# Value products of a hybrid trunk: two 144-column products joined into one of 288, the low part copied and added behind

## The chip, the cores and the metric

The kernel runs on one core of a Trainium2 chip. The metric is the device time of one execution in microseconds (us); lower is better. TensorE (PE) multiplies, VectorE (DVE), ScalarE (ACT) and GpSimd (POOL) do the elementwise work, SyncE (SP) starts the DMA transfers.

## The reference

A trunk of two layers with 2048 channels over 256 frames, with 16 learned tokens put ahead of them: T = 272 tokens. Layer 0 runs gated linear attention (GLA: 4 heads, key width 256, value width 512) and stick-breaking attention (8 heads of width 128) side by side; layer 1 is a Mamba-2 mixer. Each layer ends in a residual sum and a layer norm. What matters here is the last product of every head of layer 0, scores times values:

```python
# GLA, in chunks of 64 tokens
scores = jnp.where(causal, einsum('bcthk,bcshk->bchts', q_dec, k_inv), 0.0)
o_intra = einsum('bchts,bcshv->bcthv', scores, v)
...                                  # state of earlier chunks: o_inter
o_gla = _rms_norm_groups(o_intra + o_inter, norm_w, GLA_HEADS) * silu(gr)
# stick-breaking, in query blocks of 128
w = jnp.where(mask, exp(log_sigmoid(z) + log_between), 0.0)
outs.append(einsum('bhqk,bhkd->bhqd', w, v))
...
o_sb = outs * silu(sr)
mix = concatenate([o_gla, o_sb]);  f = mix @ w_out
```

All of it is in float32.

## The kernel before

Every large float32 product is made of three products of rounded parts: a value is split into a high part (rounded to the type fp32r by a copy on ACT) and a low part (the rest, by a subtraction, mostly on DVE). `three` (L178 to L180) then runs high times high, weights high times activations low, and weights low times activations high, each with 128 x 128 weights and 272 columns. PSUM, in which the products accumulate, holds four buffers "pj" for projections, two buffers "po" and two banks "z" for scores.

The weights of both layers come from HBM in units of 1 MB ("raw", three buffers, started by SP). ACT makes "whi" of each half (L159), DVE or POOL "wlo" (L160), five buffers each. PE runs through these units in a fixed plan: layer 0's projections, then its output product (activations "mixh", "mixl"), then layer 1. "dtgvh" and "dtgvl" are such parts of a small weight of layer 1's step sizes, split ahead of time; `hacc` (L449) is the running sum of layer 0's output.

The attention of layer 0 is side work: generators, one a head, of which a step is put between the projections' products. A scheduler then sets the final order of the instructions on each engine from its own estimate of times and from which buffers are free, so a change in one function moves instructions elsewhere too.

A head's side work, as far as it is touched here:

- its values are turned into rows of tokens through a DMA to DRAM and back ("vt"), and split into "gvh" and "gvl", two tiles of 128 tokens each (`to_tokens`, L617 to L622); tokens that don't fit, 16 at a chunk's edge, go to a small tile "v" together with their score parts "s".
- scores are made in a bank z, copied to "spad" on ACT (GLA: a plain copy; stick-breaking: an exponential, L821) and masked on POOL (L249, three selections).
- `parts_of` (L567 to L578) splits spad into "s0h" (ACT, L572) and "s0l" (DVE, L573), 432 columns: 16 for the small tile, 272 for key tile 0 and 144 for key tile 1. Key tile 1 bears only on the last 144 tokens.
- `values` (L629 to L638) adds up one block of 128 value channels in a po buffer: for key tile 0 three products of 272 columns (gvh by s0h, gvh by s0l, gvl by s0h), for key tile 1 the same three with 144 columns into columns 128 to 272 of po, and one product of 16 columns. It is called four times in each GLA head (`mix_gla`) and once in each stick-breaking head: 24 times.
- behind it, in a GLA head, DVE multiplies po by the gate ("gu", L733) and ACT squares it for the norm ("gsq", "gs", L735 and L738); POOL adds the squares (L739). In a stick-breaking head DVE multiplies po by the gate ("sby", L838), ACT makes mixh (L839) and DVE mixl (L840). The last of these heads, number 7, ends the inputs of layer 0's output product.

Of the kernel before, what the change touches and what calls it, by code (L numbers as in the profile page):

```python
# [6 lines left out]
F32 = mybir.dt.float32  # L7
F32R = mybir.dt.float32r
AF = mybir.ActivationFunctionType
ALU = mybir.AluOpType  # L10
PSUM = bass.MemoryType.PSUM

P = 128
# [6 lines left out]
T = NM + S  # L20
# [62 lines left out]
def _wait(*tasks):  # L83
    for t in tasks:
        while not t.done:
            yield


class _Body:
# [477 lines left out]
    def parts_of(self, src, stack=None, rows=()):  # L567


        n = src.shape[-1]  # L570
        p = [self.lp.tile([P, 432], F32R, tag=t, name=self.nm(t), bufs=2)[:, :n] for t in ("s0h", "s0l")]
        self.nc.scalar.activation(p[0], src, AF.Copy)  # L572
        self.nc.vector.tensor_tensor(p[1], src, p[0].bitcast(F32), op=ALU.subtract)  # L573
        for i, r in enumerate(rows):
            a = stack[32 * i : 32 * i + 16]
            b = p[r][:16, 0:16].rearrange("p (a b) -> p a b", a=1).broadcast_to([16, a.shape[1], 16])
            self.nc.vector.tensor_copy(a, b)
        return p  # L578
# [47 lines left out]
        lp = self.lp  # L626
        return [lp.tile([P, 2, 512], F32R, tag=n, name=self.nm(n), bufs=2) for n in ("gvh", "gvl")] + [self.v2[h % 2]]

    def values(self, o, vh, vl, v2, c, sh, sl, s2):  # L629

        mm = lambda r, a, b, start=False, stop=False: self.nc.tensor.matmul(  # L631
            o[:, r], a, b, start=start, stop=stop, skip_group_check=True
        )
        for t, r, w in ((0, slice(0, T), slice(16, 288)), (1, slice(128, T), slice(288, 432))):
            mm(r, vh[:, t, c], sh[:, w], start=t == 0)
            mm(r, vh[:, t, c], sl[:, w])
            mm(r, vl[:, t, c], sh[:, w])
        mm(slice(256, T), v2[:, c], s2[:, 0, :], stop=True)  # L638

    def post_gv(self, ps, h, j):  # L640
        lp = self.lp
# [61 lines left out]
    def mix_gla(self, h):  # L703
        nc, lp = self.nc, self.lp
        act, vec, mm = nc.scalar.activation, nc.vector, nc.tensor.matmul
        q, k = self.cur["q", h], self.cur["k", h]
        v = self.cur["v", h]
        g = self.cur["r", h]
        yield from _wait(self.tasks["r", h], *[self.tasks["v", h, j] for j in (1, 3)])

        zb = self.zbank()
        for j in range(2):
            mm(zb[:, 16:288], k[:, j, 0:128], q[:, j, 0:272], start=j == 0, stop=j == 1)
        for j in range(2):
            mm(zb[:, 288:432], k[:, j, 128:256], q[:, j, 272:416], start=j == 0, stop=j == 1)
        for j in range(2):
            mm(zb[:16, 0:16], k[:, j, 256:272], q[:, j, 416:432], start=j == 0, stop=j == 1)
        yield
        s = self.spad
        act(s, zb[:, :432], AF.Copy)  # L720
        self.causal(s[:, 16:144], 128, False)
        self.causal(s[:, 288:416], 128, False)
        self.causal(s[:16, 0:16], 16, False)
        yield
        st = self.s2[h % 2]
        sh, sl = self.parts_of(s, st, (0, 0, 1))
        yield
        u = lp.tile([P, 4, T], F32, tag="gu", name=self.nm("gu"))
        sq = lp.tile([P, T], F32, tag="gsq", name=self.nm("gsq"))
        for j in range(4):  # L730
            o = self.po()
            self.values(o, *v, slice(j * P, (j + 1) * P), sh, sl, st)
            vec.tensor_tensor(u[:, j, :], o[:, :T], g[:, j, :], op=ALU.mult)  # L733
            if j == 0:
                act(sq, o[:, :T], AF.Square)  # L735
            else:
                s2 = lp.tile([P, T], F32, tag="gs2", name=self.nm("gs2"), bufs=2)
                act(s2, o[:, :T], AF.Square)  # L738
                nc.gpsimd.tensor_tensor(sq, sq, s2, op=ALU.add)  # L739
            yield  # L740
        yield
        qh, ql = self.parts_of(sq)
        yield
        ms = self.po()
        mm(ms[:, :T], self.ones_r, qh, start=True, stop=False)
        mm(ms[:, :T], self.ones_r, ql, start=False, stop=True)
        yield
        m = lp.tile([P, T], F32, tag="gs2", name=self.nm("gms"), bufs=2)
        r = lp.tile([P, T], F32, tag="grs", name=self.nm("grs"))
        vec.tensor_scalar(m, ms[:, :T], 1.0 / GDV, RMS_EPS, op0=ALU.mult, op1=ALU.add)  # L750
        act(r, m, AF.Ln)
        act(r, r, AF.Exp, scale=-0.5)
        self.newton(r, m, sq)
        yield
        mh, ml = self.mix_tile(h)
        for j in range(4):
            vec.scalar_tensor_tensor(u[:, j, :], u[:, j, :], self.col(C_GN, 4 * h + j), r, op0=ALU.mult, op1=ALU.mult)
            act(mh[:, j, :], u[:, j, :], AF.Copy)
            vec.tensor_tensor(ml[:, j, :], u[:, j, :], mh[:, j, :].bitcast(F32), op=ALU.subtract)
            yield  # L760
# [23 lines left out]
    def mix_sb(self, h, q, k, v):  # L784
        nc, lp = self.nc, self.lp
        act, vec, mm = nc.scalar.activation, nc.vector, nc.tensor.matmul
        zb = self.zbank()
        gk = dict(skip_group_check=True)

        for a, b in ((0, 0), (0, 1), (1, 0)):  # L790
            mm(zb[:, 16:288], k[:, a, 0:128], q[:, b, :], start=a == b, stop=False, **gk)
        for a, b in ((0, 0), (0, 1), (1, 0)):
            mm(zb[:, 288:432], k[:, a, 128:256], q[:, b, 128:T], start=False, stop=False, **gk)
        for a, b in ((0, 0), (0, 1), (1, 0)):
            mm(zb[:16, 0:16], k[:, a, 256:T], q[:, b, 256:T], start=False, stop=False, **gk)
        yield

        sp = e = lp.tile([P, 432], F32, tag="ge", name=self.nm("sbe"))
        act(e, zb[:, :432], AF.Abs)
        act(e, e, AF.Exp, scale=-1.0)  # L800
        act(e, e, AF.Ln, bias=self.b_one)
        vec.scalar_tensor_tensor(sp[:, :432], zb[:, :432], 0.0, e, op0=ALU.max, op1=ALU.add)
        yield
        self.causal(sp[:16, 0:16], 16, True)
        self.causal(sp[:, 16:144], 128, True)
        self.causal(sp[:, 288:416], 128, True)
        yield
        sph, spl = self.parts_of(sp, self.sp2, (0, 1))
        yield

        for s in (sph, spl):
            mm(zb[:, 16:432], self.nL_r, s[:, 16:432], start=False, stop=False, **gk)
        for s in (sph, spl):
            mm(zb[:, 144:288], self.nones_r, s[:, 288:432], start=False, stop=False, **gk)

        last = zb[:, 144:432].rearrange("p (a c) -> p a c", a=2)[:, :, 128:144]
        mm(last, self.nones_r, self.sp2, start=False, stop=False, **gk)
        mm(zb[:16, 0:16], self.nL2[:, 0, :], self.sp2[:, 0, :], start=False, stop=True, **gk)
        yield
        w = self.spad  # L820
        act(w, zb[:, :432], AF.Exp)  # L821
        self.causal(w[:, 16:144], 128, True)
        self.causal(w[:, 288:416], 128, True)
        self.causal(w[:16, 0:16], 16, True)
        yield
        s2 = self.s2[h % 2]
        wh, wl = self.parts_of(w, s2, (0, 0, 1))
        yield
        while ("sv", h) not in self.tasks:
            yield  # L830
        yield from _wait(self.tasks["sv", h], self.tasks["sr", h // 4])
        o = self.po()
        self.values(o, *v, slice(0, P), wh, wl, s2)
        yield
        j, g = h % 4, 4 + h // 4
        mh, ml = self.mix_tile(g) if j == 0 else self.mix[g]
        y = lp.tile([P, T], F32, tag="gs2", name=self.nm("sby"), bufs=2)
        vec.tensor_tensor(y, o[:, :T], self.cur["sr", h // 4][:, j, :], op=ALU.mult)  # L838
        act(mh[:, j, :], y, AF.Copy)  # L839
        vec.tensor_tensor(ml[:, j, :], y, mh[:, j, :].bitcast(F32), op=ALU.subtract)  # L840
        yield
# [637 lines left out]
```

## Time and profile before

| | |
|---|---|
| median of 3 runs | 1376.98 us (1376.84, 1376.98, 1377.29) |
| the profiled execution | 1376.89 us, span 1375.2 us |
| mean granted clock of PE in it | 0.999 |
| PE busy | 1366.5 us, 99%, 10603 products |
| weight loads of PE (PEld) | 1318.6 us, 96% |
| DVE busy | 1033.6 us, 75%, 1763 instructions |
| ACT busy | 769.9 us, 56%, 1149 instructions |
| POOL busy | 263.5 us, 19%, 253 instructions |
| DMA | 256.73 MB, mean 187 GB/s |

The span runs from the first to the last event of the profiled execution; the execution's own time is 1.7 us longer. Products are pipelined in PE, so their records overlap: what one costs is the step from the end of the product ahead to its own end. A row of the timeline gives start and duration in us, engine, line, operation, output <- inputs, shape, and in brackets an idle time ahead of it with what ended it. L12 is line 12 of the kernel.

### The profile page before, as it was taken

To read this page: it belongs to the slowest core of one execution; us is meant where nothing else is said; L and a number is where in the kernel's file an instruction comes from. 1 tells how busy PE (TensorE), PEld (TensorE's weight loads), DVE (VectorE), ACT (ScalarE), POOL (GpSimd) and SP (SyncE) were. 2 spreads that over 40 slices of the span, in tenths; PEclk is the share of its full clock that TensorE was granted. 3 is DMA by queue.
4 is the path that set the end of the run, shared out by engine and by line. 5 is a ranking of instruction groups with operands and counts; after the bars stand their busy time and mean duration, and the time that the engine had idled before them with its cause. 6 is when DMAs were issued, how large, how long until landed. Compare 5 with 4: busy or idle time off the path is not lost.

```text
span 1375.2 us, 26163 instructions
## 1 busy us (share of the span) xinstructions
PE 1366.5 (99%) x10603; PEld 1318.6 (96%) x10603; DVE 1033.6 (75%) x1763; ACT 769.9 (56%) x1149; POOL 263.5 (19%) x253
## 2 busy tenths in 40 slices
PE   9999999999999999999999999999999999999998
PEld 8999999999999999999999999899898999989986
DVE  7858576576565574568899999887877879877687
ACT  6646455355345544556587676656565655656551
POOL 0000010100001100004400143331422323133221
PEclk9999999999999999999999999999999999999999
DMA  9656446446545454554355655565645565555561
GB/s 333 198 184 196 171 162 209 157 166 208 178 155 188 149 189 166 198 168 142 137 190 172 239 203 204 180 238 184 214 173 202 185 200 218 172 196 185 184 214 62
DMA packets 61945, 256.73 MB, mean 187 GB/s; under 512 B 26176, under 2 KB 29056, under 8 KB 33408
## 3 DMA queue, kind: packets, MB, share of 16 engines
q1 hardware_dynamic: 61104, 254.27, 53.7%
q8 instruction: 83, 1.36, 0.4%
q10 hardware_dynamic: 720, 0.79, 0.2%
q14 instruction: 38, 0.31, 0.1%
HBM read 249.29 MB, written 5.74 MB: 185 GB/s over the span
## 4 chain that ended last, share of the span: by engine, by line
PE 91%; DVE 6%; issue 1%; DMA 1%; ACT 0%; POOL 0%; SPq 0%; ACTq 0%; DVEq 0%; POOLq 0%
PE pj L178 25%; PE pj L179 25%; PE pj L180 24%; PE pj L494 4%; PE pj L496 4%; PE pj L495 4%; DVE wlo L160 1%; PE po L631 1%; PE po L1255 1%; DVE M L1125 1%; DMA raw<-in_wts 0%; DVE M L1126 0%; PE po L1194 0%; DVE M L1153 0%; DVE xt L1070 0%
## 5 line engine op out<-in xcount | busy, mean ns | idle before, releaser
L178 PE MATMUL pj<-xhi,whi 128*128 128x272 f32 (+4 forms) x2560 | 732.1, 286 | 1.2 <-DVE fix L956 0.5
L179 PE MATMUL pj<-xlo,whi 128*128 128x272 f32 (+4 forms) x2560 | 730.5, 286 | 0.0
L180 PE MATMUL pj<-xhi,wlo 128*128 128x272 f32 (+4 forms) x2560 | 729.8, 285 | 0.0
L159 ACT ACTIVATE whi<-raw 128x1024 fp32r<-128x1024 f32 (+2 forms) x434 | 449.2, 1038 | 379.9 <-PE pj L179 315.2
L160 DVE TENSOR_TENSOR wlo<-raw,whi 128x1024 fp32r<-128x1024 f32 (+2 forms) x405 | 503.7, 1248 | 197.5 <-ACT whi L159 192.0
L178 PEld LDWEIGHTS pj<-xhi,whi 128*128 128x128 f32 x2560 | 481.9, 188 | 3.7 <-ACT whi L159 1.5
L179 PEld LDWEIGHTS pj<-xlo,whi 128*128 128x128 f32 x2560 | 482.0, 188 | 1.7 <-issue 0.6
L180 PEld LDWEIGHTS pj<-xhi,wlo 128*128 128x128 f32 x2560 | 482.2, 188 | 0.4 <-issue 0.4
L178 PE MATMUL pj<-mixh,whi 128*128 128x272 f32 x384 | 110.9, 290 | 0.0
L180 PE MATMUL pj<-mixh,wlo 128*128 128x272 f32 x384 | 110.5, 288 | 0.0
L179 PE MATMUL pj<-mixl,whi 128*128 128x272 f32 x384 | 110.4, 288 | 0.0
L160 POOL TENSOR_TENSOR wlo<-raw,whi 128x1024 fp32r<-128x1024 f32 x29 | 73.7, 2541 | 190.5 <-ACT whi L159 175.7
L494 PE MATMUL pj<-whi,yh 128*128 128x512 f32 (+1 forms) x240 | 93.2, 388 | 0.0
L495 PE MATMUL pj<-wlo,yh 128*128 128x512 f32 (+1 forms) x240 | 92.6, 386 | 0.0
L496 PE MATMUL pj<-whi,yl 128*128 128x512 f32 (+1 forms) x240 | 92.2, 386 | 0.0
L261 POOL TENSOR_TENSOR gr<-gr,gsc 128x1088 f32<-128x1088 f32 x6 | 15.4, 2572 | 302.7 <-ACT gsc L260 302.7
L179 PEld LDWEIGHTS pj<-mixl,whi 128*128 128x128 f32 x384 | 72.4, 188 | 0.2
L178 PEld LDWEIGHTS pj<-mixh,whi 128*128 128x128 f32 x384 | 72.1, 188 | 0.4 <-ACT mixh L839 0.2
L180 PEld LDWEIGHTS pj<-mixh,wlo 128*128 128x128 f32 x384 | 72.3, 188 | 0.0
L503 DVE SCALAR_TENSOR_TENSOR acc<-pj,rr,acc 128x512 f32<-128x512 f32 (+1 forms) x65 | 46.5, 734 | 13.7 <-PE pj L496 13.5
L496 PEld LDWEIGHTS pj<-whi,yl 128*128 128x128 f32 x240 | 45.1, 188 | 9.1
L494 PEld LDWEIGHTS pj<-whi,yh 128*128 128x128 f32 x240 | 45.1, 188 | 8.9
(345 smaller groups left out, 1454.3 us busy)
## 6 DMA issues: line engine op xcount, KB each, us to landing
raw<-in_wts SPq DMA_DIRECT2D x212, 1024.0 KB, 4.9
ebc<-edr SPq DMA_DIRECT2D x8, 1664.0 KB, 6.6
raw<-in_wts SPq DMA_DIRECT2D x9, 256.0 KB, 5.9
vdr<-vt SPq DMA_DIRECT2D x8, 256.0 KB, 4.7
vt<-vdr SPq DMA_DIRECT2D x32, 64.0 KB, 2.4
hacc<-in_xT SPq DMA_DIRECT2D x7, 272.0 KB, 5.3
early<-in_wts SPq DMA_DIRECT2D x2, 512.0 KB, 6.4
vdr<-vt SPq DMA_DIRECT2D x8, 128.0 KB, 3.5
```

The lines of the kernel that those rows point to most:

```text
L159: self.nc.scalar.activation(hi, src, AF.Copy)
L160: eng.tensor_tensor(lo, src, hi.bitcast(F32), op=ALU.subtract)
L178: mm(ps, whi, xhi, start=first, stop=False)
L179: mm(ps, whi, xlo, start=False, stop=False)
L180: mm(ps, wlo, xhi, start=False, stop=last)
L261: mul(c, c, e, op=ALU.mult)
L494: mm(ps, yh[:, kk, tt], hi[:, k, :], start=kk == 0, stop=False)
L495: mm(ps, yh[:, kk, tt], lo[:, k, :], start=False, stop=False)
L496: mm(ps, yl[:, kk, tt], hi[:, k, :], start=False, stop=kk == 3)
L503: self.nc.vector.scalar_tensor_tensor(a, ps, r[:, t : t + 1], a, op0=ALU.mult, op1=ALU.add)
L631: mm = lambda r, a, b, start=False, stop=False: self.nc.tensor.matmul(o[:, r], a, b, start=start, stop=stop, skip_group_check=True)
L1125: vec.tensor_scalar(M[:, h, 0:256], eb[:, h, 0:256], self.est[:, 0, 0, gh : gh + 1], 0.0, op0=ALU.subtract, op1=ALU.min)
```

## The change

In `values`, key tile 1's two products with gvh as weights, one by the high and one by the low scores, become one product of 2 x 144 = 288 columns. Its output goes to two pieces of the po buffer: the high scores' part to columns 128 to 272 as before, the low scores' part to columns 368 to 512. Then ACT copies the low part to a tile "vlo" (one buffer), and DVE adds it to columns 128 to 272 of po. So that one operand holds both score parts, `parts_of` puts them in the two halves of one tile "s0" in place of two tiles. The area that is kept for dynamic DMA descriptors is set to 128.

```diff
     def parts_of(self, src, stack=None, rows=()):
-        p = [self.lp.tile([P, 432], F32R, tag=t, name=self.nm(t), bufs=2)[:, :n] for t in ("s0h", "s0l")]
+        p = self.lp.tile([P, 2, 432], F32R, tag="s0", name=self.nm("s0"), bufs=2)[:, :, :n]
+        p = [p[:, 0, :], p[:, 1, :], p]
...
-    def values(self, o, vh, vl, v2, c, sh, sl, s2):
+    def values(self, o, vh, vl, v2, c, s, s2):
         mm = lambda r, a, b, start=False, stop=False: self.nc.tensor.matmul(
-            o[:, r], a, b, start=start, stop=stop, skip_group_check=True
+            r, a, b, start=start, stop=stop, skip_group_check=True
         )
-        for t, r, w in ((0, slice(0, T), slice(16, 288)), (1, slice(128, T), slice(288, 432))):
-            mm(r, vh[:, t, c], sh[:, w], start=t == 0)
-            mm(r, vh[:, t, c], sl[:, w])
-            mm(r, vl[:, t, c], sh[:, w])
-        mm(slice(256, T), v2[:, c], s2[:, 0, :], stop=True)
+        w = slice(16, 288)
+        mm(o[:, :T], vh[:, 0, c], s[:, 0, w], start=True)
+        mm(o[:, :T], vh[:, 0, c], s[:, 1, w])
+        mm(o[:, :T], vl[:, 0, c], s[:, 0, w])
+        two = o[:, 32:512].rearrange("p (a x) -> p a x", a=2)[:, :, 96:240]
+        mm(two, vh[:, 1, c], s[:, :, 288:432])
+        mm(o[:, 128:T], vl[:, 1, c], s[:, 0, 288:432])
+        mm(o[:, 256:T], v2[:, c], s2[:, 0, :], stop=True)
+        e = self.lp.tile([P, 144], F32, tag="vlo", name=self.nm("vlo"))
+        self.nc.scalar.activation(e, two[:, 1], AF.Copy)
+        self.nc.vector.tensor_tensor(two[:, 0], two[:, 0], e, op=ALU.add)
...
-    nc = bacc.Bacc("TRN2", target_bir_lowering=False, num_devices=1)
+    nc = bacc.Bacc("TRN2", target_bir_lowering=False, num_devices=1, dynamic_dma_scratch_size=128)
```

The three callers of `parts_of` and the two of `values` take the new forms, and lines behind `parts_of` move down by 1, those behind `values` by 6 to 7: the products are L632 now, the copy is L644, the add L645, sby L845 and mixh L846.

Over the whole program PE has 24 products fewer, ACT 24 copies and DVE 24 adds more; the orders of POOL and SP are those of before, and so is the order of layer 1.

PE, one channel block of GLA head 1 (names carry the program's own buffer numbers; x2 marks rows alike). Before:

```order
L631 MATMUL po_2175<-s0h_2066,gvh_1175 128x272
L631 MATMUL po_2175<-s0l_2067,gvh_1175 128x272
L631 MATMUL po_2175<-s0h_2066,gvl_1176 128x272
L631 MATMUL po_2175<-s0h_2066,gvh_1175 128x144
L631 MATMUL po_2175<-s0l_2067,gvh_1175 128x144
L631 MATMUL po_2175<-s0h_2066,gvl_1176 128x144
L631 MATMUL po_2175<-s_150,v_148 128x16
```

Now:

```order
L632 MATMUL po_2186<-s_229_2072,gvh_1176 128x272 x2
L632 MATMUL po_2186<-s_229_2072,gvl_1177 128x272
L632 MATMUL po_2186<-s_229_2072,gvh_1176 128x2x144
L632 MATMUL po_2186<-s_229_2072,gvl_1177 128x144
L632 MATMUL po_2186<-s_150,v_148 128x16
```

Seven products stand as six, and the two by gvh with 144 columns are the one with 2 x 144.

ACT, where stick-breaking head 7 makes its scores, between splits of weights. Before:

```order
L821 ACTIVATE spad<-z_64 128x432
L621 ACTIVATE gvh_7398<-vt_7482 128x128 x2
L159 ACTIVATE dtgvh<-dtraw 128x8x64
L617 ACTIVATE v_148<-vt_7482 16x128
L159 ACTIVATE dtgvl<-dtraw 128x8x64
L572 ACTIVATE s0h_7556<-spad 128x432
L159 ACTIVATE whi_7712<-raw_7584 128x1024
L159 ACTIVATE whi_7758<-raw_7662 128x1024
L839 ACTIVATE mixh_6865<-sby_7644 128x272
```

Now:

```order
L622 ACTIVATE gvh_7422<-vt_7505 128x128 x2
L828 ACTIVATE spad<-z_64 128x432
L159 ACTIVATE dtgvh<-dtraw 128x8x64
L618 ACTIVATE v_148<-vt_7505 16x128
L159 ACTIVATE dtgvl<-dtraw 128x8x64
L573 ACTIVATE s_920_7579<-spad 128x432
L159 ACTIVATE whi_7736<-raw_7606 128x1024
L159 ACTIVATE whi_7782<-raw_7686 128x1024
L644 ACTIVATE vlo_7647<-po_7640 128x144
L846 ACTIVATE mixh_6889<-sby_7668 128x272
```

The exponential into spad moved behind the two copies of gvh, and the copy vlo stands ahead of mixh.

DVE, at the end of the same head. Before:

```order
L449 TENSOR_TENSOR hacc<-hacc,pj_7648 128x272
L160 TENSOR_TENSOR wlo_7759<-raw_7662,whi_7758 128x1024
L838 TENSOR_TENSOR sby_7644<-po_7618,gr_6317 128x272
L840 TENSOR_TENSOR mixl_6866<-sby_7644,mixh_6865 128x272
L449 TENSOR_TENSOR hacc<-hacc,pj_7668 128x272
```

Now:

```order
L449 TENSOR_TENSOR hacc<-hacc,pj_7672 128x272
L160 TENSOR_TENSOR wlo_7783<-raw_7686,whi_7782 128x1024
L645 TENSOR_TENSOR po_7640<-po_7640,vlo_7647 128x144
L845 TENSOR_TENSOR sby_7668<-po_7640,gr_6341 128x272
L847 TENSOR_TENSOR mixl_6890<-sby_7668,mixh_6889 128x272
L449 TENSOR_TENSOR hacc<-hacc,pj_7692 128x272
```

The add L645 stands between wlo and sby; the sum L449 ahead of that wlo and mixl behind sby keep their places.

Elsewhere in layer 0 the third and fourth channel blocks of the GLA heads stand 10 to 20 products later in PE's order than before.

More of the change, by code (lines that the diff above doesn't have):

```diff
@@ L725, in mix_gla @@
         st = self.s2[h % 2]
-        sh, sl = self.parts_of(s, st, (0, 0, 1))
+        sp = self.parts_of(s, st, (0, 0, 1))[2]
         yield
@@ L731, in mix_gla @@
             o = self.po()
-            self.values(o, *v, slice(j * P, (j + 1) * P), sh, sl, st)
+            self.values(o, *v, slice(j * P, (j + 1) * P), sp, st)
             vec.tensor_tensor(u[:, j, :], o[:, :T], g[:, j, :], op=ALU.mult)
@@ L741, in mix_gla @@
         yield
-        qh, ql = self.parts_of(sq)
+        qh, ql, _ = self.parts_of(sq)
         yield
@@ L807, in mix_sb @@
         yield
-        sph, spl = self.parts_of(sp, self.sp2, (0, 1))
+        sph, spl, _ = self.parts_of(sp, self.sp2, (0, 1))
         yield
@@ L826, in mix_sb @@
         s2 = self.s2[h % 2]
-        wh, wl = self.parts_of(w, s2, (0, 0, 1))
+        wp = self.parts_of(w, s2, (0, 0, 1))[2]
         yield
@@ L832, in mix_sb @@
         o = self.po()
-        self.values(o, *v, slice(0, P), wh, wl, s2)
+        self.values(o, *v, slice(0, P), wp, s2)
         yield
```

## The prediction

> **What bounds the kernel now.** I read the page's busy times first, then the shares of the chain that ended last, then the view of the waits of TensorE (PE): what it waits for, in total, how often, the longest.
>
> ```profile
> span 1375.2 us, 26163 instructions
> PE 1366.5 (99%) x10603; PEld 1318.6 (96%) x10603; DVE 1033.6 (75%) x1763; ACT 769.9 (56%) x1149; POOL 263.5 (19%) x253
> PE 91%; DVE 6%; issue 1%; DMA 1%; ACT 0%; POOL 0%; SPq 0%; ACTq 0%; DVEq 0%; POOLq 0%
> PE pj L178 <- ACT whi L159: 0.4, 2, 0.3
> ```
>
> PE is busy 99% of the span and carries 91% of the chain; the last row is one of seven that the waits of PE have, and they sum to some 4 us. So an edit counts by what PE's stream gets shorter, and by any new wait of PE. VectorE (DVE) and ScalarE (ACT) have a quarter and almost half of their time free: work there costs only where PE is just waiting for it.
>
> One group of value products, in PE's timeline, with the product ahead and two behind:
>
> ```profile
> 98.39 0.28 PE L180 MATMUL pj<-xhi,wlo 128*128 128x272 f32 x1
> 98.51 0.29 PE L631 MATMUL po<-s0h,gvh 128*128 128x272 f32 x1
> 98.63 0.29 PE L631 MATMUL po<-s0l,gvh 128*128 128x272 f32 x1
> 98.76 0.29 PE L631 MATMUL po<-s0h,gvl 128*128 128x272 f32 x1
> 98.89 0.23 PE L631 MATMUL po<-s0h,gvh 128*128 128x144 f32 x1
> 98.95 0.27 PE L631 MATMUL po<-s0l,gvh 128*128 128x144 f32 x1
> 99.06 0.28 PE L631 MATMUL po<-s0h,gvl 128*128 128x144 f32 x1
> 99.18 0.22 PE L631 MATMUL po<-s,v 80*128 80x16 f32 x1
> 99.25 0.37 PE L178 MATMUL pj<-xhi,whi 128*128 128x272 f32 x1
> 99.46 0.29 PE L179 MATMUL pj<-xlo,whi 128*128 128x272 f32 x1
> ```
>
> Start plus duration is the end; products overlap, so the step from end to end is what one costs. The ends are 98.67, 98.80, 98.92, 99.05, 99.12, 99.22, 99.34, 99.40, 99.62, 99.75. Steps: 0.13, 0.12, 0.13 for 272 columns; 0.07, 0.10, 0.12 for the three of 144; 0.06 for 16; then 0.22 instead of 0.125. A product behind a short one steps as if about 0.11 had to pass first, whatever its columns: I take it for the weights, which can't be loaded faster.
>
> **The change, part by part.**
>
> PE: the rows of one channel block, before and now, stand in the section on the change. Seven products become six; the columns stay 1264. Removed: the steps of three products of 144, 0.07 + 0.10 + 0.12 = 0.29. In their place: 288 columns, 288/272 x 0.125 = 0.13, then one 144 behind a long one, 0.07: 0.20. Gain 0.09 a group, 24 groups (16 in the four GLA heads, 8 in the stick-breaking heads): 2.2 us. That an output in two pieces costs nothing extra I bound by the nearest row, the 2x16 product of L817: its 0.22 is that of the plain 16 columns above. The other end is a product that pays the 0.11 for each piece, 0.22 + 0.07 = 0.29, no gain.
>
> ```profile
> 569.67 0.22 PE L817 MATMUL z<-sp,nones 128*128 128x32 f32 x1
> ```
>
> Added: 24 copies 128x144 on ACT, 24 adds 128x144 on DVE. Nearest rows:
>
> ```profile
> L562 ACT ACTIVATE ke<-ge 128x128 f32<-128x128 f32 x8 | 2.4, 303 | 0.8 <-DVE ge L554 0.8
> L679 DVE SCALAR_TENSOR_TENSOR gq<-pj,qe 128x144 f32<-128x144 f32 x8 | 2.4, 297 | 0.0
> ```
>
> About 0.3 each, 7 us on either engine over 550 us, covered by their free time. One buffer holds the copy, so the next copy waits for the add; each gate or stick-breaking product, and so the release of the accumulator, comes some 0.7 later. In 23 groups nobody on PE is near: the third rival prices it. One tile with two halves instead of s0h and s0l frees both at once, a little later for one of them than before. The view of L572 shows how often such a pair is made (count, durations, first and last start):
>
> ```profile
> L572 ACT ACTIVATE s0h<-spad x12: 547/550/566, 88.2 to 632.8; 128x432 fp32r<-128x432 f32 x12
> L572 ACT ACTIVATE s0h<-sbe x8: 545/566/567, 435.2 to 624.7; 128x432 fp32r<-128x432 f32 x8
> L572 ACT ACTIVATE s0h<-gsq x4: 430/432/433, 109.4 to 379.9; 128x272 fp32r<-128x272 f32 x4
> ```
>
> 24 pairs in 545 us, 16 of them in the 198 us from 435: one in 12 us there, with two buffers, so nobody is near that. The smaller scratch area for DMAs moves no product. SP and POOL issue what they issued, in the same order, so the weights' transfers meet nothing new. I cost the three at nothing; what covers them is that distance, and if it were gone, a score part would come some 0.3 later in each head.
>
> The 24th group is stick-breaking head 7, after which layer 0's last output products start. There PE already waits:
>
> ```profile
> 629.36 1.25 POOL L249 TENSOR_SCALAR_AFFINE_SELECT spad<-spad 128x128 f32<-128x128 f32 x3 [4.70 <-ACT spad L821]
> 628.71 0.52 ACT L821 ACTIVATE spad<-z 128x432 f32<-128x432 f32 x1
> 631.18 0.51 ACT L621 ACTIVATE gvh<-vt 128x128 fp32r<-128x128 f32 x2 [1.95 <-DMA vt<-vdr]
> 631.60 0.62 ACT L159 ACTIVATE dtgvh<-dtraw 128x512 fp32r<-128x512 f32 x1
> 632.84 0.55 ACT L572 ACTIVATE s0h<-spad 128x432 fp32r<-128x432 f32 x1
> 632.28 0.68 DVE L160 TENSOR_TENSOR dtgvh<-dtraw,dtgvh 128x512 fp32r<-128x512 f32 x1
> 637.53 1.22 DVE L160 TENSOR_TENSOR wlo<-raw,whi 128x1024 fp32r<-128x1024 f32 x1
> 638.66 0.43 DVE L838 TENSOR_TENSOR sby<-po,gr 128x272 f32<-128x272 f32 x1
> 639.13 0.43 ACT L839 ACTIVATE mixh<-sby 128x272 fp32r<-128x272 f32 x1 [3.72 <-DVE sby L838]
> 633.91 0.29 PE L631 MATMUL po<-s0h,gvh 128*128 128x272 f32 x1
> 637.73 0.18 PE L631 MATMUL po<-s,v 80*128 80x16 f32 x1
> 639.62 0.55 PEld L178 LDWEIGHTS pj<-mixh,whi 128*128 128x128 f32 x4 [0.22 <-ACT mixh L839]
> ```
>
> The bracket on a row is the idle time ahead of it and what ended it. PE's last value product ended at 637.91, but DVE was in its wlo until 638.75; sby, then mixh, then PE's weights at 639.62. DVE has no idle mark from 632.28 to here. The order shown with the change moves two things into this chain. On ACT, the copy of the stick-breaking weights to spad (L821, now L828) stood ahead of the two gvh copies and now stands behind them, and they wait for the DMA that brings vt, as the mark of 1.95 at 631.18 says. On DVE, sby followed wlo directly; now the add of the low part (L645) stands between them.
>
> In before's times: spad starts at 631.60 and, with the usual 0.1 of overlap, puts dtgvh off by 0.43, and so DVE's dtgvh and everything behind it. spad's selections on POOL end at 632.12 + 0.13 + 1.25 = 633.50, the score part at 634.09 instead of 633.39, and PE's first value product at 633.91 waits some 0.3. DVE's wlo ends at 638.75 + 0.43 = 639.18; the copy is long there (PE's last product near 638.2); the add takes 0.3 less overlap, sby starts near 639.43, mixh ends at 640.33, PE goes on at 640.39: 0.77 later than 639.62, with the 0.3 above inside it. Bounds: 0 if the DMA lands early enough and the add hides, 1.2 if the add costs as sby does and the copy is late. What follows is fed by this point, so it carries to the end; this group's own 0.09 is lost in the wait.
>
> Sum: 1376.89 (the profiled execution: span 1375.2 and 1.7 around it; the median, 1376.98, lies 0.09 higher) - 23 x 0.09 (2.1) + 0.8 = 1375.6; with 0.095 a group, which the two-decimal steps of the other groups lean to, 1375.4. I take 1375.5, 0.1% faster.
>
> **The rivals.**
>
> Columns alone: a product costs its columns, the change removes 288 and adds 288, and PE gains nothing; or the two pieces pay twice. Then 1376.9 + 0.8 = 1377.7. The steps 0.10 and 0.12 against 0.07 for equal columns speak against it. [...]
>
> Head 7 doesn't wait longer: 1376.9 - 2.2 = 1374.7, or 1374.2 if its old wait goes too and each group gains 0.1. For it: only a DMA landing, 631.18, set the shift.
>
> Slower: the accumulator is handed over late. There are two buffers; the third and fourth blocks of a GLA head need those of the first two, which now wait for copy, add and gate.
>
> ```profile
> 171.37 0.44 DVE L733 TENSOR_TENSOR gu<-po,gr 128x272 f32<-128x272 f32 x1 [0.27 <-PE po L631]
> 171.84 0.40 ACT L738 ACTIVATE gs<-po 128x272 f32<-128x272 f32 x1 [0.31 <-DVE gu L733]
> 176.11 1.06 ACT L159 ACTIVATE whi<-raw 128x1024 fp32r<-128x1024 f32 x1 [0.31 <-PE pj L179]
> ```
>
> Now a whi stands ahead of that second gs and could hold it, with the third block. But the order also puts 44 products (5.4 us) between second and third block where 22 stood, so I find the buffers free 2 to 3 us early. It decides once PE waits over 0.5 at each of these 8 hand-overs (8 x 0.5 outweighs the gain of 1.4 and the 2.75 of the bound); at 1 us each, 1383.5.
>
> **How the numbers follow.** 0.2% is 2.75 us, about what a measurement of this kernel can tell from no change. Forecast 0.55, columns alone 0.12, head 7 free 0.18, late hand-over 0.10, unnamed 0.05. Faster than 1374.2 needs the best end of the third case and some of the unnamed: 0.13. Slower than 1379.7: the hand-over and the rest: 0.12. Same: 0.75. Range 1373.9 to 1378.4: from the free head 7 at its best, less 0.3 for the runs, to columns alone with head 7 at its bound of 1.2 (1378.1) and 0.3 for the runs; outside lie the late hand-over and most of the unnamed.
>
> **What would show it.** In the new profile: 24 products 128x288 stepping 0.13, groups of about 0.73 instead of 0.82; PE's wait for mixh near 638 grown from 0.2 to about 0.9; no wait of PE on po; DVE's row for L645 and ACT's for L644 near 0.3 each, 24 times. Wrong if the 288 steps 0.2 or more, or if PE waits for gs or gu.

## The result and the profile after

The changed kernel takes 1373.15 us (median of 9 runs, 1372.70 to 1374.36), the kernel before 1376.84 (9 runs, 1376.36 to 1377.30): ratio 0.9975, 95% interval 0.9967 to 0.9983. That is 3.7 us less, where 1.4 less had been forecast, and 0.75 below the low end of the range. The changed kernel was profiled twice; the first profiled execution took 1374.36, the second 1374.08. The rows below are from the first. Sums and mean steps are taken from the trace's own times, which are finer than the hundredths of the printed rows.

The page of the changed kernel, busy times and shares of the chain:

```profile
span 1372.6 us, 26176 instructions
PE 1362.9 (99%) x10579; PEld 1315.7 (96%) x10579; DVE 1041.2 (76%) x1787; ACT 775.8 (57%) x1173; POOL 259.2 (19%) x253
PE 91%; DVE 6%; issue 1%; DMA 1%; POOL 0%; ACT 0%; SPq 0%; ACTq 0%; DVEq 0%; POOLq 0%
```

PE still bounds it. Its 24 products fewer stand against 24 instructions more on DVE and on ACT (7.6 and 5.9 us of busy time).

The group of value products that answers to the one shown of before, in PE's timeline of the changed kernel:

```profile
98.72 0.29 PE L180 MATMUL pj<-xhi,wlo 128*128 128x272 f32 x1
98.85 0.42 PE L632 MATMUL po<-s,gvh 128*128 128x272 f32 x2
99.11 0.29 PE L632 MATMUL po<-s,gvl 128*128 128x272 f32 x1
99.23 0.30 PE L632 MATMUL po<-s,gvh 128*128 128x288 f32 x1
99.36 0.23 PE L632 MATMUL po<-s,gvl 128*128 128x144 f32 x1
99.43 0.22 PE L632 MATMUL po<-s,v 80*128 80x16 f32 x1
99.50 0.38 PE L178 MATMUL pj<-xhi,whi 128*128 128x272 f32 x1
```

The ends are 99.01, 99.27, 99.40, 99.53, 99.59, 99.65 and 99.88. The joined product steps 0.13, the 144 columns behind it 0.06. Over all 24 groups, with what the next product steps beyond its columns, the sum is 17.64 us (0.735 a group); the same sum over the trace of before is 19.84 (0.827). The change's own part is worth 2.2 us, 0.09 a group.

The rest lies between the groups. PE's timeline in a stretch that holds nothing but layer 0's output product, before:

```profile
510.01 0.29 PE L179 MATMUL pj<-mixl,whi 128*128 128x272 f32 x1
510.14 0.29 PE L180 MATMUL pj<-mixh,wlo 128*128 128x272 f32 x1
510.26 0.29 PE L178 MATMUL pj<-mixh,whi 128*128 128x272 f32 x1
510.39 0.29 PE L179 MATMUL pj<-mixl,whi 128*128 128x272 f32 x1
510.52 0.29 PE L180 MATMUL pj<-mixh,wlo 128*128 128x272 f32 x1
510.65 0.29 PE L178 MATMUL pj<-mixh,whi 128*128 128x272 f32 x1
510.77 0.29 PE L179 MATMUL pj<-mixl,whi 128*128 128x272 f32 x1
```

and after:

```profile
510.02 0.29 PE L179 MATMUL pj<-mixl,whi 128*128 128x272 f32 x1
510.14 0.28 PE L180 MATMUL pj<-mixh,wlo 128*128 128x272 f32 x1
510.26 0.29 PE L178 MATMUL pj<-mixh,whi 128*128 128x272 f32 x1
510.39 0.28 PE L179 MATMUL pj<-mixl,whi 128*128 128x272 f32 x1
510.51 0.29 PE L180 MATMUL pj<-mixh,wlo 128*128 128x272 f32 x1
510.63 0.28 PE L178 MATMUL pj<-mixh,whi 128*128 128x272 f32 x1
510.76 0.29 PE L179 MATMUL pj<-mixl,whi 128*128 128x272 f32 x1
```

From the first start to the last, the same six products take 0.76 us before and 0.74 after; over the whole stretch it is 0.1267 and 0.1234 a product. Before, every record is 0.29 long; after, 0.29 and 0.28 alternate. The finer times say the same: before, every step is 0.126 or 0.127; after, a step of 0.121 or 0.122 follows each one of 0.125 or 0.126. In the rest of layer 0 both kernels step 0.1234, but for a few runs of under ten products. I call a run at the other pace a slow stretch. The trace of before has three: 440.3 to 444.8 (36 products), 505.4 to 557.8 (414) and 570.0 to 574.4 (36). 486 products at 0.0033 more are 1.6 us; the trace after has under 0.1 of it, in short runs. The long one begins right behind the value group of stick-breaking head 3:

```profile
504.95 0.27 PE L631 MATMUL po<-s0l,gvh 128*128 128x144 f32 x1
505.06 0.28 PE L631 MATMUL po<-s0h,gvl 128*128 128x144 f32 x1
505.17 0.22 PE L631 MATMUL po<-s,v 80*128 80x16 f32 x1
505.24 0.37 PE L178 MATMUL pj<-mixh,whi 128*128 128x272 f32 x1
505.45 0.29 PE L179 MATMUL pj<-mixl,whi 128*128 128x272 f32 x1
505.58 0.29 PE L180 MATMUL pj<-mixh,wlo 128*128 128x272 f32 x1
```

The two others begin in the same way behind the score products of heads 0 and 4.

The view by windows counts it (columns: stretch, its length, then busy us and number of instructions of PE, PEld, DVE, ACT and POOL, the granted clock, the DMA share and GB/s). Before:

```profile
510.00:550.00 40.00, 40.00 (x318) 40.00 (x317) 20.54 (x24) 17.21 (x17) 2.57 (x1) 1.00 0.50 168
```

After:

```profile
510.00:550.00 40.00, 40.00 (x327) 40.00 (x326) 21.35 (x24) 17.82 (x18) 2.56 (x1) 1.00 0.56 193
```

318 products in 40 us against 327, at a granted clock of 1.00 in both. "PE 100% busy" hides it: the records overlap, so a slower step looks no less busy. The DMA share does not part the two paces: kernels below that run this window at the fast pace have 0.51 and 0.52 there, beside 0.50 here.

With 2.2 from the groups, 1.6 from the stretches and 0.1 lost at head 7 (below), the sum is 3.7. The end of layer 0 shows it: of PE's products on hacc that follow, the row of eight starts at 722.24 before and at 718.71 after, 3.5 earlier, and in the second traces at 721.64 and 718.50, 3.1 earlier.

### The profile page after: what moved, and what is told of

Read it like the earlier page. It is cut to its first block, busy times and chain, and to the rows that moved or that the text cites. A ratio compares the mean times of both kernels' runs of the same rounds, so it can differ in the third digit from the quotient of the medians.

```text
span 1372.6 us, 26176 instructions
## 1 busy us (share of the span) xinstructions
PE 1362.9 (99%) x10579; PEld 1315.7 (96%) x10579; DVE 1041.2 (76%) x1787; ACT 775.8 (57%) x1173; POOL 259.2 (19%) x253
## 4 chain that ended last, share of the span: by engine, by line
PE 91%; DVE 6%; issue 1%; DMA 1%; POOL 0%; ACT 0%; SPq 0%; ACTq 0%; DVEq 0%; POOLq 0%
PE pj L178 25%; PE pj L179 24%; PE pj L180 24%; PE pj L494 4%; PE pj L496 4%; PE pj L495 4%; DVE wlo L160 1%; PE po L1262 1%; PE po L632 1%; DVE M L1132 1%; DMA raw<-in_wts 0%; DVE M L1133 0%; PE po L1201 0%; DVE M L1160 0%; DVE xt L1077 0%
```

## Experiments

Every time is the median of 9 to 11 runs beside the kernel before on the same chip, which took 1376.7 to 1376.8 in each of the three sets; two kernels ran once only and are marked so. The interval of each ratio, in brackets, is about 1.2 us wide to either side, so a median alone gives little more than the sign of a change; the sizes rest on the traces, one execution each.

**The change's storage alone.** `parts_of` as in the change, its two views p[0] and p[1] used as before, and the smaller descriptor area:

```diff
-        p = [... lp.tile([P, 432], F32R, tag=t, ...) for t in ("s0h", "s0l")]
+        p = self.lp.tile([P, 2, 432], F32R, tag="s0", name=self.nm("s0"), bufs=2)[:, :, :n]
+        p = [p[:, 0, :], p[:, 1, :]]
...
+ ... dynamic_dma_scratch_size=128
```

> The kernel before with the change's storage alone: the two score parts in one tile and the smaller descriptor area; products, copies and their order on every engine are those of before. In the trace of before, three stretches (440.3 to 444.8, 505.4 to 557.8, 570.0 to 574.4) run at 0.1267 us per product of 272 columns instead of 0.1234, together 1.6 us; after the change they are gone. Theory A (a gait of TensorE that a run of short products leaves behind): 1376.8, the same three stretches at the same places. Theory B (where operands lie in memory): 1375.2, no such stretches. Theory C (chance of one execution): 1376.8, stretches elsewhere or none.

Measured: 1375.38, ratio 0.9990 (0.9981 to 0.9999). With not one instruction added, removed or moved, 1.4 us went. The three stretches are gone, and a new one of 0.8 us stands at 639.7 to 669.9. That explains 0.8 of the 1.4; the rest is within the interval and stays open. So theory A, as I had put it (the products alone decide), is wrong for this run, and B, as put (operands decide and no stretch is left), too: storage counts, but it can make a stretch as well as end one. The window of this kernel over the old place:

```profile
510.00:550.00 40.00, 40.00 (x327) 40.00 (x326) 21.58 (x25) 17.61 (x18) 2.58 (x1) 1.00 0.53 181
```

and over the new one:

```profile
642.00:667.00 25.00, 25.00 (x200) 25.00 (x199) 23.71 (x29) 14.66 (x30) 22.94 (x23) 1.00 0.49 170
```

where the kernel before has more products:

```profile
642.00:667.00 25.00, 25.00 (x205) 25.00 (x204) 24.25 (x29) 15.54 (x31) 22.89 (x21) 1.00 0.46 154
```

**One small product more.** In the value group of stick-breaking head 3 alone, behind which the long stretch begins:

```diff
+        if nudge:                      # h == 3
+            mm(slice(400, 416), v2[:, c], s2[:, 0, :])
         mm(slice(256, T), v2[:, c], s2[:, 0, :], stop=True)
```

> The kernel before with one more product of 16 columns into unused columns of the accumulator, ahead of the last product of the value group of stick-breaking head 3, behind which the long slow stretch (505.4 to 557.8) begins. Nothing else moves on any engine. Theory A (a gait set by the short products just ahead): the stretch goes, 1.4 less 0.1 for the added product, 1375.5. Theories B (operands' places) and C (chance): 1376.9 to 1377.0, the stretch stays or lies elsewhere.

Measured: 1375.05, ratio 0.9989 (0.9980 to 0.9998): a kernel with more work is 1.7 faster. The stretch behind head 3 is gone, the two others stand where they were. PE's wait of 0.22 for mixh at head 7 is missing in this execution.

```profile
510.00:550.00 40.00, 40.00 (x326) 40.00 (x326) 21.58 (x24) 17.18 (x18) 2.57 (x1) 1.00 0.51 177
```

**The joined product in the GLA heads alone, and in the stick-breaking heads alone.** The other heads call a copy of the old `values` on the halves of the one tile; the storage is that of the change.

```diff
-        self.values(o, *v, slice(0, P), wp, s2)
+        self.values_old(o, *v, slice(0, P), wp, s2)
```

(for the GLA heads alone; for the other kernel the call in `mix_gla` is changed instead.)

> The joined product in the 16 groups of the GLA heads alone, the stick-breaking heads with seven products as before. The joined product gains 16 x 0.085 = 1.4. If the slow stretches stay (they lie in the stick-breaking part, whose products are those of before): 1375.4. If a shift in what comes ahead is enough to end them: 1373.9. Theory of the prediction (groups alone, no gait): 1375.4.

> The joined product in the 8 groups of the stick-breaking heads alone. Gain of the groups 8 x 0.085 = 0.7. Theory A (gait set by the short products just ahead): the stretch behind head 3 goes too, 1374.8; the two behind the score products of heads 0 and 4 may stay or go (0.25). No gait: 1376.1. In either, PE's wait for mixh at head 7 stays at 0.3 or less.

Measured: GLA alone 1374.30, ratio 0.9981 (0.9973 to 0.9990); stick-breaking alone 1374.62, ratio 0.9984 (0.9975 to 0.9993). Both exceed what their groups can give, and the two gains (2.5 and 2.2) add up to more than the whole change's 3.7. The traces part it. GLA alone: its 16 groups 13.22 to 11.76 us, a gain of 1.5; slow stretches 1.6 to 0.8 (the old three gone, one at 638.2 to 668.3). Stick-breaking alone: its 8 groups 6.62 to 5.88, a gain of 0.7; slow stretches 1.6 to under 0.1. Groups gain 0.09 each, a little more than the 0.085 of the expectations; the remainder is the stretches. GLA heads alone:

```profile
642.00:667.00 25.00, 25.00 (x200) 25.00 (x199) 22.91 (x28) 14.64 (x29) 23.02 (x22) 1.00 0.46 165
```

and stick-breaking heads alone:

```profile
642.00:667.00 25.00, 25.00 (x205) 25.00 (x204) 23.39 (x29) 14.60 (x30) 23.02 (x23) 1.00 0.48 169
```

So in every kernel with the storage of the change the old three are gone, whatever its products, and the new one near 640 is absent from each that has the joined product in the stick-breaking heads.

**The score parts in one tile, and nothing else.** As the first experiment, without the smaller descriptor area, so that all other tiles lie where they lay.

```diff
+        p = self.lp.tile([P, 2, 432], F32R, tag="s0", name=self.nm("s0"), bufs=2)[:, :, :n]
+        p = [p[:, 0, :], p[:, 1, :]]
```

> The kernel before with only the two score parts laid into one tile: the order on every engine is that of before, and all other tiles lie where they lay (the smaller descriptor area of the first experiment, which moved every tile down by 16256 bytes, is not taken). If the places of the score parts decide where TensorE falls into the slow gait: 1375.4, as the first experiment, no stretch at 440, 505 and 570. If the shift of all tiles decides: 1376.8, three stretches as before.

Measured: 1375.13, ratio 0.9989 (0.9980 to 0.9997). No stretch is left:

```profile
510.00:550.00 40.00, 40.00 (x326) 40.00 (x326) 21.57 (x24) 17.17 (x17) 2.58 (x1) 1.00 0.52 175
```

The four tiles (two buffers of each part) fill the same bytes in both kernels; the one tile sets high, low, high, low in a row where there was high, high, low, low, so that only the first low and the second high buffer changed places. The order of every engine is that of before, and PE's waits sum to within 0.2 of what they were; this is what tells the two kernels apart, and it is worth 1.7 us by the medians and 1.6 by the traces. Against it the changed kernel, 2.0 faster by the medians, shows the joined product's own worth, without a stretch in either: 2.2 in the groups, less some 0.1 at head 7.

**The smaller descriptor area alone.**

> The kernel before with the smaller descriptor area alone: every tile lies 16256 bytes lower, the two score parts stay in two tiles, the order is that of before. If only the places of the score parts against each other matter: the three stretches of before, 1376.8. If the shift made the new stretch at 639.7 to 669.9 of the first experiment: that one too, 1377.5. If any move of tiles draws new stretches: others, 1375 to 1378.

Measured: 1377.06, ratio 1.0000 (0.9990 to 1.0009). The three stretches are at 440.6, 505.7 and 570.2, each as long as before: moving every tile by the same 16256 bytes changes nothing here.

```profile
510.00:550.00 40.00, 40.00 (x318) 40.00 (x317) 20.53 (x24) 17.21 (x17) 2.54 (x1) 1.00 0.50 166
```

The new stretch of the first experiment therefore needs both, the one tile and the shift. Why is open.

**A small product more at each of the three places.** The 16 columns at head 3 as above, and at the score products of heads 0 and 4:

```diff
+        if h in (0, 4):
+            mm(zb[:, 440:472], self.nones_r, self.sp2, start=False, stop=False, **gk)
         mm(zb[:16, 0:16], self.nL2[:, 0, :], self.sp2[:, 0, :], start=False, stop=True, **gk)
```

> The kernel before with a small added product ahead of the last one at each of the three places behind which a slow stretch begins: 32 columns into unused columns at the score products of stick-breaking heads 0 and 4, and 16 columns at the value group of head 3 as in the second experiment. Nothing else moves. If the short products just ahead set the gait: all three stretches go, 1.6 less 0.3 for the added products, 1375.4, near the kernel with the score parts in one tile. If not: 1377.1.

Measured: 1374.95, ratio 0.9987 (0.9978 to 0.9996). All three stretches are gone, none is new:

```profile
510.00:550.00 40.00, 40.00 (x326) 40.00 (x325) 21.57 (x25) 17.21 (x18) 2.56 (x1) 1.00 0.52 176
```

**The kernel before once more** (one run).

> The kernel before, unchanged, profiled once more. If the slow stretches belong to the program: 440.3 to 444.8, 505.4 to 557.8 and 570.0 to 574.4 again, 1.6 us in all, at 1376.8. If each execution draws them by chance: elsewhere, or none, and a time between 1375.2 and 1377.

Measured: 1376.07, with the stretches at 440.0 to 444.4, 505.1 to 557.4 and 569.6 to 574.1, of 36, 414 and 36 products again. They come with the program and not by chance, though this execution ran 0.3 ahead of the first from its first microseconds on.

```profile
510.00:550.00 40.00, 40.00 (x318) 40.00 (x318) 20.54 (x24) 17.22 (x17) 2.57 (x1) 1.00 0.50 172
```

**No copy, no add.** The changed kernel without L644 and L645.

> The changed kernel without the copy to vlo and without the add: the low part of key tile 1 is left out of the sum. It prices copy and add together. Theory of the prediction (hidden in all groups but at the last head): PE's wait for mixh near 636 falls from 0.32 to nothing, 0.3 less than the changed kernel, 1372.9, the six products of each group stepping as before. Rival (the accumulators are handed over late in the GLA heads): 2 or more less, 1371. A new slow stretch of TensorE can add 0.1 to 1.5 to either, and shows in the profile as 0.1267 per product.

Measured: 1373.45, ratio 0.9976 (0.9966 to 0.9986), no less than the changed kernel. With the intervals as wide as they are, a difference under 1 us would not show in the medians. The groups sum to 17.67, PE's wait for mixh is gone, and no accumulator was late. In the traces of layer 0 copy and add cost hardly more than the 0.3 of that wait. The edit moves more than it removes: the scheduler puts the third and fourth blocks of the GLA heads back to back again, 23 projection products behind the second, where the changed kernel has 44.

**The changed kernel once more** (one run).

> The changed kernel, profiled once more. Its first profiled execution took 1374.36, 1.2 more than the median, with a wait of PE of 1.4 for POOL's ysq near 841, where before had 0.4. If that wait is of one execution: 0.4 or less this time, and 1373.2; no slow stretch over 0.1 us. If it belongs to the changed kernel: 1.4 again and 1374.3.

Measured: 1374.08, no slow stretch, and the wait of 1.4 again: it was not of one execution. In the first trace it is the longest of PE's waits (it ends at 833.6):

```profile
PE po L1288 <- POOL ysq L1282: 1.4, 1, 1.4
```

It goes back to ACT, which some 25 us earlier stood idle for a unit of weights:

```profile
807.55 1.06 ACT L159 ACTIVATE whi<-raw 128x1024 fp32r<-128x1024 f32 x1 [0.99 <-DMA raw<-in_wts]
```

ACT, DVE and POOL are 1.05 later from there on, and at POOL's sum for layer 1's norm PE meets it. The second trace has 1.01 at the same unit; the trace of before and that of the kernel without copy and add, which was as early there, have no wait for it. In both profiled executions 1.05 of the gain is lost here, and both are about 1 above the median. That the other executions don't have this wait would explain the median, but none of them was profiled: it is open, and so is whether the copy and the add bring the wait about.

## Why the prediction was wrong

The step that failed is a term that the prediction put at nothing. It named the one tile for both score parts and the smaller descriptor area, and costed them at nothing, covered by the distance between the pairs of score parts. That distance covers waits of PE for buffers, and none came. It does not cover the pace of PE, which the prediction took as fixed outside the value groups without saying so, reading "busy 99%" and seven waits of some 4 us as the whole of what PE loses. The one tile alone, with no instruction moved, is worth 1.7 us (1.6 in the trace): 1.6 us of before lay in slow stretches that waits don't show. The rows were there: products of 272 columns stepping 0.1267 from 505.4 on, against 0.1234 elsewhere. Of the 3.7 us, 2.2 are the groups and 1.6 the stretches, less 0.1 at head 7. That the change's storage ends the three stretches, and that no new one comes near 640, is luck: nothing in the change aimed at it.

- Groups: right. 0.09 a group had been forecast, 2.1 in 23 groups; measured 0.09, 2.2 in 24. The two-piece output costs nothing extra: 24 joined products average 0.132 but for one of 0.24 that stands behind a product of 16 columns, and 288/272 x 0.1234 is 0.131. The prediction's bound for it compared the lengths of two records (0.22), which are not steps.
- Columns alone: wrong, as weighed. It would have the groups gain nothing; the traces have 2.2. That the loading of the weights sets the step of a short product behind a short one was the author's reading, and the trace of before agrees with it: in its first 640 us no two loads of 128 x 128 weights start less than 0.108 apart (4983 pairs), beside steps of 0.109 to 0.116 for 144 columns behind 144 in the value groups. That the loads are the cause no run here shows.
- Late hand-over: did not happen. PE waits on po for neither gu nor gs, with the 44 products that the order puts ahead of the third block; how it would go without them the runs don't show.
- Copy and add hidden: right. The copy took 0.29 and the add 0.31 where 0.3 each had been taken from the nearest rows. Four times ACT sat idle until an add had read the one buffer, 3.0 us in all; no wait of PE goes back to it.
- Head 7: the term of 0.8 was mis-sized, it is 0.1 (PE waits 0.32 for mixh instead of 0.22); the rival that had it free was the nearer one. ACT, DVE, the weight load of PE and the last transfer's issue there in the changed kernel:

```profile
624.55 0.55 SPq L609 DMA_DIRECT2D vt<-vdr  x1
626.09 0.62 ACT L622 ACTIVATE gvh<-vt 128x128 fp32r<-128x128 f32 x2 [0.79 <-DMA vt<-vdr]
626.61 0.51 ACT L828 ACTIVATE spad<-z 128x432 f32<-128x432 f32 x1
632.93 1.22 DVE L160 TENSOR_TENSOR wlo<-raw,whi 128x1024 fp32r<-128x1024 f32 x1
634.46 0.29 ACT L644 ACTIVATE vlo<-po 128x144 f32<-128x144 f32 x1 [2.56 <-PE po L632]
634.78 0.32 DVE L645 TENSOR_TENSOR po<-po,vlo 128x144 f32<-128x144 f32 x1 [0.63 <-ACT vlo L644]
635.61 0.43 ACT L846 ACTIVATE mixh<-sby 128x272 fp32r<-128x272 f32 x1 [0.86 <-DVE sby L845]
636.09 0.54 PEld L178 LDWEIGHTS pj<-mixh,whi 128*128 128x128 f32 x4 [0.32 <-ACT mixh L846]
```

and the same issue before:

```profile
628.10 0.55 SPq L608 DMA_DIRECT2D vt<-vdr  x1
```

gvh started 1.54 us after the issue of the last small transfer, where before it was 3.08 (631.18 less 628.10). The sum had the spad copy, which now stands behind gvh, at 631.60; PE had gained 3.5 by then, so that is 628.1 in the new times, and the copy started at 626.61, 1.5 earlier. DVE was therefore through its wlo at 634.15, ahead of the end of PE's last value product (634.40), where before it had been 0.84 behind it. Copy, add, sby and mixh then ran one behind the other, and PE waited 0.32 where it had waited 0.22. The sum had taken the landing from the one execution of before as given; the second execution of before has no wait for mixh at all. Beside the 3.08 of before, the kernel with the smaller descriptor area alone has 2.86 there (628.38 to 631.24) and the one with a small product more at three places 2.16 (626.99 to 629.15); why is open.

With head 7 at 0.1, all 24 groups and the stretches put in, the prediction's own sum gives 1376.9 - 2.2 + 0.1 - 1.6 = 1373.2, beside 1373.15 measured.

## What to carry to other kernels

Where TensorE is busy throughout, read its steps, from end to end, and not its busy share: where two stretches of like products step unlike, a change nearby can give or take that time (here 1.6 us) without meaning to, and a gain of such a size has to be told from the change's own by a kernel with the change's layout alone. Two short products by the same weights are worth joining into one when the second steps longer than its columns (here 0.11 where 144 columns step 0.067 behind a long product, and 0.09 a group won). The copy and the add that this costs took 0.29 and 0.31 each here, on engines busy 57% and 76% of the span; in layer 0 PE waited for a sum at one place alone, head 7, 0.32 where it had waited 0.22.

## What the runs showed of the hardware

In these kernels TensorE has two paces for the same products at the same granted clock of 1.00: 0.1234 and 0.1267 us for 272 columns with 128 x 128 weights. In the fast one every other step is shorter (0.121 or 0.122 beside 0.125 or 0.126, from 510 to 550 in the changed kernel); in the slow one all are 0.126 or 0.127 (the same window before). In the trace of before it took up the slow one behind a run of short products, three times; in two kernels (the storage alone, the GLA heads alone) behind a single long step in layer 0's last output products, where two loads of weights start 0.20 apart (639.29 and 639.49, 637.75 and 637.95). The traces of before, of the changed kernel, of the smaller descriptor area alone and of the small product at three places have a step of 0.18 to 0.19 there too; in them, and in the six others, the window of 642 to 667 has 205 products, the fast pace, where the two have 200. The slow pace lasted over hundreds of products by ever new weights (414 in 52 us), and in the trace of before it ended where products of another kind came between: one of L631 at 444.9 and at 574.5, two of L791 at 557.9. Which pace follows was the same in each execution of a program that was profiled (two of before, with 318 products from 510 to 550, and two of the changed kernel, with 327 and 326; the shifted copy has the 318 of before), and changed when a product of 16 columns was added (326) or when two buffers of its operands changed places (326). What sets it inside TensorE no run here shows.
